# q and k of a forgetting-attention layer projected token-major and turned through DRAM, in a two-layer trunk on one core

## The chip, the cores and the metric

The kernel runs on one core of one Trainium2 chip. The metric is the device time of one execution in microseconds (us), of which three runs are given. A profiled execution is shown besides; its span runs from its first to its last instruction.

## The reference, cut to what matters

Two layers over 256 tokens of width 2048, in float32. Layer 0 mixes tokens with an mLSTM of 4 heads, layer 1 with FoX, a softmax attention of 16 heads of 128 whose logits carry a cumulative log-forget-gate. Each mixer and each SwiGLU feed-forward part (inner width 5632) is preceded by an RMSNorm with a scale and a shift from a conditioning vector, and added to the residual with a gate from the same vector. The part that the change touches:

```python
def fox_mixer(h, w_in, b_f, w_out):
    proj = h @ w_in
    q, k, v, fl = jnp.split(proj, [D_MODEL, 2 * D_MODEL, 3 * D_MODEL], axis=-1)
    heads = lambda a: a.reshape(B, T, Hh, FOX_HEAD_DIM).transpose(0, 2, 1, 3)
    log_f = jax.nn.log_sigmoid(fl + b_f).transpose(0, 2, 1)
    o = forgetting_attention(heads(q), heads(k), heads(v), log_f)
    return o.transpose(0, 2, 1, 3).reshape(B, T, D_MODEL) @ w_out

# forgetting_attention, per head:
#   s = q @ k.T * dh**-0.5 + cum[t] - cum[s], causal;  out = softmax(s) @ v
# swiglu:  (silu(g) * u) @ w_down,  g, u = split(h @ w_gate_up)
```

## The kernel before

All large products run in a split form: a float32 tile is written as hi + lo, both in the fast format of TensorE, and hi·hi, hi·lo and lo·hi are summed in PSUM. Weights come from DRAM in tiles of 4 x 128 rows by 512 columns (1 MB, `fetch`, line 250). For each, `split` (255) lets ScalarE (ACT) cast hi and VectorE (DVE) subtract lo, two 128x1024 pieces each. `raw` tiles have 5 buffers, hi and lo 4 each, so two tiles can be split ahead of TensorE.

Two forms of group multiply the 256 tokens by 512 columns over 16 tiles of the inner dimension:

- `group_a` (316), the plain form. Tokens are stationary, weights move. For each inner tile and each half of the tokens `mm_t` (285) issues three matmuls of 512 columns (lines 288 to 290), 96 a group, into two PSUM banks. The result is token-major: partitions are tokens.
- `group_b` (296), used for q and k of the FoX layer alone. Weights are stationary, activations move. For each inner tile and each of four blocks of 128 output features `mm_b` (269) issues a matmul of 512 columns (line 271; the activation's hi and lo side by side) and one of 256 (line 274), 128 a group, into four banks. The result is feature-major, as attention wants q and k. `total` (366) adds the two halves of each bank: a copy on ACT (368), an add on DVE (370 or 372).

After each weight tile comes a `tick` (245): it runs `adv` waiting steps from the list `steps` and then `bg(n)`, which adds n to a credit. A whole unit of credit fetches a further 1 MB tile of `ada_w` on SP's queue and lets DVE multiply it with the conditioning vector (line 193, the ada products). Weight fetches are on SP's queue too. So one tick is one weight tile: 24 plain matmuls, or 32 of `group_b`. Apart from stretches ordered by hand, the order on each engine is drawn up at compile time from the program order and from what is ready by the compiler's own timing.

The FoX stage (line 1213 on) finishes the v projections begun before, computes the gates, and then runs four iterations (1293): two `group_b` for q and k of four heads, with the v groups of columns 1024 and 1536 ahead of iterations 1 and 2. A head has three steps: *scores* (logit bias, mask and q·k on TensorE, lines 691, 696 and 1229; row maximum on DVE, exponential on ACT, scaling on DVE, line 1251), *flip* (three TensorE transposes of the weights, 958, and their copy on ACT, 959) and *mix* (weights by v, 1261 and 1264, and the split of the result into `y`). The steps of four heads are interleaved and run during the following groups, one a tick, or two a tick in a v group and in the output projection. What is left when the next four heads are added is run at once by `drain`. `project_out` (1093) then runs three plain groups on `y`, running out the steps ahead of the inner tiles from 12 on; the fourth group is in `bridge`.

In the feed-forward parts the products silu(g)·u are token-major and are needed feature-major. One way is by TensorE (`turned`, 342). Where `lag` is set (line 1153: the second chunk of layer 0, both of layer 1) the way is through DRAM: `blocks` (352) has DVE transpose every 32x32 block of a 128x512 tile (353) and POOL write it to `aside` in DRAM (357); `gather` (359) has POOL read it back in four transfers (361) so that each partition holds one feature of each of four blocks; after `lag` ticks, a step `flip` (1165) reads it and casts hi on ACT (1171) and subtracts lo on DVE (1172). In that layout the four feature blocks lie inside, so both read every fourth element.

Tiles of 128x1024 float32 (`slot`) share 16 buffers.

Of the kernel before, what the change touches and what calls it, by code (L numbers as in the profile page):

```python
# [31 lines left out]
def kernel(  # L32
# [26 lines left out]
    def bank():  # L59
        return psum.tile([P, 512], F32, tag="mm", name=nm("mm"))  # L60
# [7 lines left out]
    def t256():  # L68
        return t512()[:, :T]
# [169 lines left out]
    def drain(n=None):  # L239
        if steps:  # L240
            settle()
        for _ in range(len(steps) if n is None else min(n, len(steps))):
            steps.pop(0)()

    def tick(n, adv=1):
        drain(adv)
        grow_all()
        bg(n)
# [17 lines left out]
        raw = fetch(w, k0, nk, c0)  # L266
        return [p for j in range(0, nk, 2) for p in split(raw, j)]

    def mm_b(ps, hi, lo, rhs, first, last):
        def big():  # L270
            nc.tensor.matmul(ps, hi, rhs, start=first, stop=last, skip_group_check=True)  # L271

        def little():
            nc.tensor.matmul(  # L274
                ps[:, T:], lo, rhs[:, :T], start=False, stop=False, skip_group_check=True
            )

        if last:
            little()
            big()  # L280
        else:
            big()
            little()

    def mm_t(ps, hi, lo, act, t, first, last):
        a = act[:, t * P : (t + 1) * P]
        b = act[:, T + t * P : T + (t + 1) * P]
# [4 lines left out]
    def mm_a(ps, hi, lo, act, first, last):  # L292
        for t in range(2):
            mm_t(ps[t], hi, lo, act, t, first, last)

    def group_b(w, nk, c0, act, evac, bgn, adv=1):
        banks = [bank() for _ in range(4)]
        for k in range(0, nk, 4):
            ws = load_w(w, k, 4, c0)
            for m in range(4):  # L300
                cols = slice(m * P, (m + 1) * P)
                for j, (hi, lo) in enumerate(ws):
                    mm_b(
                        banks[m], hi[:, cols], lo[:, cols], act(k + j), k + j == 0, k + j == nk - 1
                    )
                if k + 4 == nk:
                    evac(m, banks[m])
            tick(bgn, adv)

    late = []  # L310

# [39 lines left out]

    def blocks(dst, src, aside):
        nc.vector.transpose(  # L353
            dst.rearrange("p (j b m) -> p j m b", j=4, m=4),
            src.rearrange("p (m j b) -> p j m b", m=4, j=4),
        )
        nc.gpsimd.dma_start(aside, dst)  # L357

    def gather(whole, aside):
        for j in range(4):  # L360
            nc.gpsimd.dma_start(
                whole[32 * j : 32 * j + 32].rearrange("a (g b) m -> a g (b m)", b=32),
                aside.rearrange("t (i a) c -> a (t i) c", a=32)[:, :, j * P : (j + 1) * P],
            )

    def total(ps, out, scale=None):
        b = t256()
        nc.scalar.activation(b, ps[:, T:], AF.Copy, scale=1.0 if scale is None else scale)
        if scale is None:
            nc.vector.tensor_tensor(out, ps[:, :T], b, op=ALU.add)  # L370
        else:
            nc.vector.scalar_tensor_tensor(
                out=out, in0=ps[:, :T], scalar=scale, in1=b, op0=ALU.mult, op1=ALU.add
            )

    def split_act(src, dst):
        nc.scalar.copy(dst[:, :T], src)
# [673 lines left out]
    def interleave(*lists):  # L1051
        return [f for fs in zip(*lists) for f in fs]

    def keep_t(c0, bgn, scale=None, adv=1, layer_w=0):
        if layer_w == 0:
            i = COLS.index(c0)
            unit(i, start[i], KT, bgn)
            sp = SP[i]
            o = slot().rearrange("p (k t) -> p k t", t=T)

            def flip():
                for i in range(2):
                    nc.scalar.copy(o[:, 2 * i : 2 * i + 2, :], turned(sp, i))

            steps.append(flip)
            return o
        o = slot().rearrange("p (k t) -> p k t", t=T)
        group_b(w, KT, c0, h_act, lambda m, ps: total(ps, o[:, m, :], scale), bgn, adv)
        return o

    for i in range(1, 4):
        unit(i, start[i], KT, LR[0])
# [19 lines left out]

    def project_out(wo, res, bgn, adv, upto, norm, w2, heads):
        act = lambda k: act_tile(y, k)
        for i in range(3):
            res.both(i, group_a(
                wo, 512 * i, act, bgn, adv, before=lambda k: drain() if k >= upto else None
            ))
        return bridge(wo, 0, KT, 1536, act, res, 3, norm, w2, heads)

# [10 lines left out]
    def ffn(layer, begun, norm, rates, nsplit=0, srate=0.0, nxt=None):  # L1111
# [36 lines left out]
        def swiglu(gr, lag):  # L1148
            sg = pair(slot())
            banks = column(512 * gr)  # L1150
            for t in range(2):
                nc.scalar.activation(sg[:, t, :], banks[t], AF.Silu)
            banks = column(DFF + 512 * gr)
            for t in range(2):
                nc.vector.tensor_tensor(sg[:, t, :], banks[t], sg[:, t, :], op=ALU.mult)
            first = len(acts)
            acts.extend([None, None])
            if lag:
                whole = slot().rearrange("p (t m) -> p t m", m=4)
                aside = dram.tile([2, P, 512], F32, tag="aside", name=nm("aside"))  # L1160
                for t in range(2):
                    blocks(t512(), sg[:, t, :], aside[t])
                gather(whole, aside)

            def flip(i):
                acts[first + i] = dst = new_act()
                if lag:
                    ps = whole[:, :, 2 * i : 2 * i + 2].rearrange("p t m -> p m t")
                else:
                    ps = turned(sg, i)  # L1170
                nc.scalar.copy(dst[:, :, :T], ps)  # L1171
                nc.vector.tensor_tensor(  # L1172
                    dst[:, :, T:], ps, dst[:, :, :T].bitcast(F32), op=ALU.subtract
                )

            steps.extend([lambda: None] * lag)
            steps.extend([lambda: flip(0), lambda: flip(1)])
# [43 lines left out]
    def fox_head(hd, q, k):  # L1221
        st = {}

        def scores():
            S = abank()
            logits(u3, hd, S, False)
            for t in range(2):
                n = P * (t + 1)
                nc.tensor.matmul(  # L1229
                    S[:, T * t : T * t + n], q[:, t * P : (t + 1) * P], k[:, :n],  # L1230
                    start=False, stop=t == 1, skip_group_check=True,
                )
            mx = small([P, 2], "den", bufs=4)
            buf = slot()
            W = buf[:, : 3 * P]
            st["W"], st["WT"] = W, buf[:, 512 : 512 + 3 * P]
            sm = small([P, 2], "r", bufs=4)
            for t in range(2):
                nc.vector.tensor_reduce(
                    out=mx[:, t : t + 1], in_=S[:, slice(*causal[t])], axis=AX.X, op=ALU.max,  # L1240
                    negate=True,
                )
            for t in range(2):
                nc.scalar.activation(
                    W[:, slice(*packed[t])], S[:, slice(*causal[t])], AF.Exp,
                    bias=mx[:, t : t + 1], accum_out=sm[:, t : t + 1],
                )
            nc.vector.reciprocal(sm, sm)
            for t in range(2):
                wt = W[:, slice(*packed[t])]  # L1250
                nc.vector.tensor_scalar(wt, wt, sm[:, t : t + 1], None, op0=ALU.mult)

        def flip():
            weights_t(st["W"], st["WT"])

        def mix():
            v, WT = vals[hd // 4][:, :, hd % 4 * P : (hd % 4 + 1) * P], st["WT"]
            if hd % 2 == 0:
                y[hd // 2] = new_act()
            O = abank()  # L1260
            nc.tensor.matmul(
                O[:, :T], v[:, 0, :], WT[:, :T], start=True, stop=False, skip_group_check=True
            )
            nc.tensor.matmul(
                O[:, P:T], v[:, 1, :], WT[:, T:], start=False, stop=True, skip_group_check=True
            )
            split_act(O[:, :T], act_tile(y, hd))

        return [scores, flip, mix]
# [22 lines left out]
    u3 = split3(cum, 16, new)  # L1292
    for i in range(4):
        if i == 1:
            vals[2] = keep_v(group_a(w, 2 * D + 1024, h_act, FR, ka=12, banks=begun[2 * D + 1024]))
        if i == 2:
            vals[3] = keep_v(group_a(w, 2 * D + 1536, h_act, FR, 2))
        q = keep_t(512 * i, FR, P ** -0.5, layer_w=1)
        k = keep_t(D + 512 * i, FR, layer_w=1)
        drain()  # L1300
        steps.extend(interleave(*[
            fox_head(4 * i + j, q[:, j, :], k[:, j, :]) for j in range(4)
        ]))
    res = Residual(1, G1, True)
    norm = Norm(res, 1, SC2, SH2)
    begun = project_out(fox_out, res, FR, 2, 12, norm, gate_up[1], [0, DFF, 512])
# [116 lines left out]
```

## Time and profile before

| | |
|---|---|
| runs | 2279.60, 2282.02, 2283.16 us (median 2282.02) |
| profiled execution | 2279.4 us, span 2277.6 us |
| granted TensorE clock, mean | 0.999 |
| TensorE matmul busy | 2255.0 us (99%) |
| TensorE weight load busy | 1848.2 us (81%) |
| VectorE, ScalarE, GpSimd busy | 1653.0, 1139.6, 71.2 us |
| moved by DMA | 640.69 MB, mean 281 GB/s |

The page lists engines as PE (matmul), PEld (weight load, which overlaps PE), DVE, ACT, POOL and SP. A row of a group gives line, engine, operation, what it writes and reads with shapes, the count, busy us, mean ns of one, then the engine's idle time ahead of it and what ended it. Matmul durations overlap; the distance between starts tells the rate. A row of the waits gives who waited for whom, us in total, times and the longest.

### The profile page before, as it was taken

To read this page: it belongs to the slowest core of one execution; us is meant where nothing else is said; L and a number is where in the kernel's file an instruction comes from. 1 tells how busy PE (TensorE), PEld (TensorE's weight loads), DVE (VectorE), ACT (ScalarE), POOL (GpSimd) and SP (SyncE) were. 2 spreads that over 40 slices of the span, in tenths; PEclk is the share of its full clock that TensorE was granted. 3 is DMA by queue.
4 is the path that set the end of the run, shared out by engine and by line. 5 is a ranking of instruction groups with operands and counts; after the bars stand their busy time and mean duration, and the time that the engine had idled before them with its cause. 6 is when DMAs were issued, how large, how long until landed. Compare 5 with 4: busy or idle time off the path is not lost.

```text
span 2277.6 us, 26530 instructions
## 1 busy us (share of the span) xinstructions
PE 2255.0 (99%) x10250; PEld 1848.2 (81%) x10250; DVE 1653.0 (73%) x1865; ACT 1139.6 (50%) x1493; POOL 71.2 (3%) x136
## 2 busy tenths in 40 slices
PE   8999999999999999999999999999999999999998
PEld 5877878888888888888888888887888888888886
DVE  7998789878887878875687777777665555555564
ACT  4778564555543344444555444455444443444443
POOL 1000000000000000100000000000100100010000
PEclk9999999999999999999999999999999999999999
DMA  9998989788888889996667877675777665566662
GB/s 394 371 369 321 353 307 354 283 338 334 325 335 330 326 335 349 360 350 219 217 238 288 299 273 277 250 274 189 271 276 255 221 204 189 201 223 219 206 233 98
DMA packets 93571, 640.69 MB, mean 281 GB/s; under 512 B 11443, under 2 KB 11891, under 8 KB 19077
## 3 DMA queue, kind: packets, MB, share of 16 engines
q1 hardware_dynamic: 86400, 617.79, 73.5%
q0 software_dynamic: 6896, 21.08, 3.1%
q8 instruction: 80, 1.31, 0.2%
q14 instruction: 47, 0.38, 0.0%
q10 hardware_dynamic: 148, 0.14, 0.0%
HBM read 628.44 MB, written 10.52 MB: 281 GB/s over the span
## 4 chain that ended last, share of the span: by engine, by line
PE 87%; DVE 5%; DMA 4%; ACT 2%; issue 1%; POOL 0%; SPq 0%; ACTq 0%; DVEq 0%; POOLq 0%
PE mm L289 25%; PE mm L290 25%; PE mm L288 25%; PE mm L271 5%; PE mm L274 3%; DMA ada<-in_ada_w_dram 3%; DVE lo L262 2%; DVE ada L193 2%; ACT hi L261 1%; DMA slot<-in_w_in_dram 1%; PE aux L1010 0%; PE aux L498 0%; PE aux L1229 0%; PE mm L569 0%; PE mm L565 0%
## 5 line engine op out<-in xcount | busy, mean ns | idle before, releaser
L262 DVE TENSOR_TENSOR lo<-raw,hi 128x1024 fp32r<-128x1024 f32 x764 | 924.2, 1221 | 470.8 <-ACT hi L261 469.5
L261 ACT CAST hi<-raw 128x1024 fp32r<-128x1024 f32 x764 | 796.9, 1054 | 870.7 <-PE mm L290 742.2
L289 PE MATMUL mm<-lo,hT 128*128 128x512 f32 x1846 | 720.3, 390 | 3.3 <-DVE lo L262 3.2
L290 PE MATMUL mm<-hi,hT 128*128 128x512 f32 x1846 | 719.8, 390 | 0.0
L288 PE MATMUL mm<-hi,hT 128*128 128x512 f32 x1846 | 719.1, 392 | 0.0
L193 DVE SCALAR_TENSOR_TENSOR ada<-ada,cs 128x2048 f32<-128x2048 f32 x192 | 438.7, 2285 | 55.7 <-DMA ada<-in_ada_w_dram 55.3
L289 PEld LDWEIGHTS mm<-lo,hT 128*128 128x128 f32 x1846 | 346.7, 188 | 78.5 <-DVE lo L262 7.4
L290 PEld LDWEIGHTS mm<-hi,hT 128*128 128x128 f32 x1846 | 346.5, 188 | 72.4 <-issue 0.5
L288 PEld LDWEIGHTS mm<-hi,hT 128*128 128x128 f32 x1846 | 346.5, 188 | 71.9 <-issue 0.5
L288 PE MATMUL mm<-hi,slot 128*128 128x512 f32 x960 | 375.0, 391 | 0.2 <-ACT slot L1043 0.2
L289 PE MATMUL mm<-lo,slot 128*128 128x512 f32 x960 | 374.2, 390 | 0.2 <-DVE lo L262 0.2
L290 PE MATMUL mm<-hi,slot 128*128 128x512 f32 x960 | 374.1, 390 | 0.0
L288 PEld LDWEIGHTS mm<-hi,slot 128*128 128x128 f32 x960 | 180.3, 188 | 38.0 <-ACT slot L1043 0.8
L290 PEld LDWEIGHTS mm<-hi,slot 128*128 128x128 f32 x960 | 180.2, 188 | 37.7 <-issue 0.7
L289 PEld LDWEIGHTS mm<-lo,slot 128*128 128x128 f32 x960 | 180.2, 188 | 37.5 <-DVE lo L262 0.6
L271 PE MATMUL mm<-hT,hi 128*128 128x512 f32 x512 | 181.5, 401 | 0.0
L274 PE MATMUL mm<-hT,lo 128*128 128x256 f32 x512 | 138.4, 281 | 0.4 <-DVE lo L262 0.4
L271 PEld LDWEIGHTS mm<-hT,hi 128*128 128x128 f32 x512 | 94.4, 188 | 19.6
L274 PEld LDWEIGHTS mm<-hT,lo 128*128 128x128 f32 x512 | 96.6, 189 | 4.1 <-DVE lo L262 1.1
L865 ACT ACTIVATE slot<-mm 128x512 f32<-128x512 f32 x78 | 45.3, 596 | 39.7 <-PE mm L290 37.9
L357 POOL DMA_DIRECT2D aside<-t x32 | 18.0, 562 | 1239.7 <-DVE t L353 1239.7
L1172 DVE TENSOR_TENSOR slot<-slot,slot 128x512 fp32r<-128x512 f32 x32 | 34.8, 1090 | 24.8 <-ACT slot L1171 24.8
(220 smaller groups left out, 1049.6 us busy)
## 6 DMA issues: line engine op xcount, KB each, us to landing
ada<-in_ada_w_dram SPq DMA_DIRECT2D x192, 1024.0 KB, 6.3
raw<-in_gate_up_dram SPq DMA_DIRECT2D x176, 1024.0 KB, 5.2
raw<-in_down_dram SPq DMA_DIRECT2D x88, 1024.0 KB, 4.9
raw<-in_fox_in_dram SPq DMA_DIRECT2D x48, 1024.0 KB, 4.9
raw<-in_w_in_dram SPq DMA_DIRECT2D x44, 1024.0 KB, 7.2
raw<-in_w_out_dram SPq DMA_DIRECT2D x16, 1024.0 KB, 5.8
raw<-in_fox_out_dram SPq DMA_DIRECT2D x16, 1024.0 KB, 4.9
aside<-t POOLq DMA_DIRECT2D x32, 256.0 KB, 2.5
```

Of the source, the lines that this page charges most:

```text
L193: nc.vector.scalar_tensor_tensor(out=raw, in0=raw, scalar=1.0, in1=cs, op0=ALU.mult, op1=ALU.mult, accum_out=acc[layer][:, j : j + 1],)
L261: nc.scalar.copy(hi, raw[:, j : j + 2, :])
L262: nc.vector.tensor_tensor(lo, raw[:, j : j + 2, :], hi.bitcast(F32), op=ALU.subtract)
L271: nc.tensor.matmul(ps, hi, rhs, start=first, stop=last, skip_group_check=True)
L274: nc.tensor.matmul(ps[:, T:], lo, rhs[:, :T], start=False, stop=False, skip_group_check=True)
L288: nc.tensor.matmul(ps, a, hi, start=first, stop=False, skip_group_check=True)
L289: nc.tensor.matmul(ps, a, lo, start=False, stop=False, skip_group_check=True)
L290: nc.tensor.matmul(ps, b, hi, start=False, stop=last, skip_group_check=True)
L357: nc.gpsimd.dma_start(aside, dst)
L865: nc.scalar.activation(SP[i][:, t, :], banks[t], func)
L1172: nc.vector.tensor_tensor(dst[:, :, T:], ps, dst[:, :, :T].bitcast(F32), op=ALU.subtract)
```

## The change

- q and k of the FoX layer are projected by `group_a`. `group_b`, `mm_b` and `total` are gone. ACT copies the two banks out (for q with the factor 1/sqrt(128)), `blocks` and `gather` take them through DRAM into a slot.
- The layout in DRAM and in that slot is now (group of 32 tokens, feature block, token), so that a feature block is read in runs of 32 tokens, 128 elements apart (`tiles`). The feed-forward flips use the same helpers and read such runs too.
- k's slot is read by the score matmul as it lies. q, which is stationary there, is copied on ACT into another slot.
- A list `timed` holds functions with the tick at which they are due. The copy of q is due 6 ticks after the last tick of its k group (4 in the last iteration), which is 10 after its own; the heads' steps are added one tick later, two heads after two heads, and run two a tick. So the heads of iteration i run during the groups of iterations i + 1 and i + 2.
- The v group of columns 1536 comes after the four iterations.
- In the FoX output projection the first two groups run over the inner tiles 0 to 11 first, while the last four heads run, and then over 12 to 15.

```diff
     def blocks(dst, src, aside):
         nc.vector.transpose(
-            dst.rearrange("p (j b m) -> p j m b", j=4, m=4),
+            dst.rearrange("p (j m b) -> p j m b", j=4, m=4),
...
-                whole[32 * j : 32 * j + 32].rearrange("a (g b) m -> a g (b m)", b=32),
+                whole[32 * j : 32 * j + 32].rearrange("a (g c) -> a g c", c=P),
...
+    def tiles(whole):
+        return whole.rearrange("p (g m b) -> p m g b", m=4, b=32)
...
     def tick(n, adv=1):
+        clock[0] += 1
+        while timed and timed[0][0] <= clock[0]:
+            timed.pop(0)[1]()
         drain(adv)
...
     def keep_t(c0, bgn, scale=None, adv=1, layer_w=0):
...
-        o = slot().rearrange("p (k t) -> p k t", t=T)
-        group_b(w, KT, c0, h_act, lambda m, ps: total(ps, o[:, m, :], scale), bgn, adv)
-        return o
+        banks = group_a(w, c0, h_act, bgn, adv)
+        whole = slot()
+        aside = dram.tile([2, P, 512], F32, tag="aside", name=nm("aside"))
+        for t in range(2):
+            own = t512()
+            nc.scalar.activation(own, banks[t], AF.Copy, scale=1.0 if scale is None else scale)
+            blocks(t512(), own, aside[t])
+        gather(whole, aside)
+        return tiles(whole)
...
     def project_out(wo, res, bgn, adv, upto, norm, w2, heads):
+        first = {}
+        if upto == 12:
+            for i in range(2):
+                first[i] = group_a(wo, 512 * i, act, bgn, adv, kb=upto, more=True)
+            assert not timed
+            drain()
         for i in range(3):
             res.both(i, group_a(
-                wo, 512 * i, act, bgn, adv, before=lambda k: drain() if k >= upto else None
+                wo, 512 * i, act, bgn, adv, ka=upto if i in first else 0, banks=first.get(i),
+                before=lambda k: drain() if k >= upto else None,
             ))
...
             def flip(i):
                 acts[first + i] = dst = new_act()
+                hi, lo = dst[:, :, :T], dst[:, :, T:]
                 if lag:
-                    ps = whole[:, :, 2 * i : 2 * i + 2].rearrange("p t m -> p m t")
+                    ps = tiles(whole)[:, 2 * i : 2 * i + 2]
+                    hi, lo = (x.rearrange("p m (g b) -> p m g b", b=32) for x in (hi, lo))
...
                 nc.tensor.matmul(
-                    S[:, T * t : T * t + n], q[:, t * P : (t + 1) * P], k[:, :n],
+                    S[:, T * t : T * t + n].rearrange("p (g b) -> p g b", b=32),
+                    q[:, t * P : (t + 1) * P], k[:, : n // 32],
...
     for i in range(4):
         if i == 1:
-            vals[2] = keep_v(group_a(w, 2 * D + 1024, h_act, FR, ka=12, banks=begun[2 * D + 1024]))
-        if i == 2:
-            vals[3] = keep_v(group_a(w, 2 * D + 1536, h_act, FR, 2))
-        q = keep_t(512 * i, FR, P ** -0.5, layer_w=1)
-        k = keep_t(D + 512 * i, FR, layer_w=1)
-        drain()
-        steps.extend(interleave(*[
-            fox_head(4 * i + j, q[:, j, :], k[:, j, :]) for j in range(4)
-        ]))
+            vals[2] = keep_v(
+                group_a(w, 2 * D + 1024, h_act, FR, 2, ka=12, banks=begun[2 * D + 1024])
+            )
+        far = keep_t(512 * i, FR, P ** -0.5, 2, layer_w=1)
+        k = keep_t(D + 512 * i, FR, None, 2, layer_w=1)
+        q = slot().rearrange("p (m t) -> p m t", t=T)
+        heads = [fox_head(4 * i + j, q[:, j, :], k[:, j]) for j in range(4)]
+
+        def begin(q=q, far=far, heads=heads):
+            nc.scalar.copy(q.rearrange("p m (g b) -> p m g b", b=32), far)
+            timed.append((clock[0] + 1, lambda: steps.extend(
+                interleave(*heads[:2]) + interleave(*heads[2:])
+            )))
+
+        timed.append((clock[0] + (LAND if i < 3 else LAND - 2), begin))
+    vals[3] = keep_v(group_a(w, 2 * D + 1536, h_act, FR, 2))
```

More of the change, by code (lines that the diff above doesn't have):

```diff
@@ L243, in drain @@
             steps.pop(0)()
+    clock = [0]
+    timed = []
     def tick(n, adv=1):
+        clock[0] += 1
+        while timed and timed[0][0] <= clock[0]:
+            timed.pop(0)[1]()
         drain(adv)
@@ L267, in load_w @@
         return [p for j in range(0, nk, 2) for p in split(raw, j)]
[L269 to L283, printed above, removed]
     def mm_t(ps, hi, lo, act, t, first, last):
@@ L294, in mm_a @@
             mm_t(ps[t], hi, lo, act, t, first, last)
[L296 to L308, printed above, removed]
     late = []
@@ L361, in gather @@
             nc.gpsimd.dma_start(
-                whole[32 * j : 32 * j + 32].rearrange("a (g b) m -> a g (b m)", b=32),
+                whole[32 * j : 32 * j + 32].rearrange("a (g c) -> a g c", c=P),
                 aside.rearrange("t (i a) c -> a (t i) c", a=32)[:, :, j * P : (j + 1) * P],
             )
[L366 to L374, printed above, removed]
+    def tiles(whole):
+        return whole.rearrange("p (g m b) -> p m g b", m=4, b=32)
     def split_act(src, dst):
@@ L1052, in interleave @@
         return [f for fs in zip(*lists) for f in fs]
+    LAND = 6
     def keep_t(c0, bgn, scale=None, adv=1, layer_w=0):
@@ L1158, in swiglu @@
             if lag:
-                whole = slot().rearrange("p (t m) -> p t m", m=4)
+                whole = slot()
                 aside = dram.tile([2, P, 512], F32, tag="aside", name=nm("aside"))
@@ L1166, in flip @@
                 acts[first + i] = dst = new_act()
+                hi, lo = dst[:, :, :T], dst[:, :, T:]
                 if lag:
-                    ps = whole[:, :, 2 * i : 2 * i + 2].rearrange("p t m -> p m t")
+                    ps = tiles(whole)[:, 2 * i : 2 * i + 2]
+                    hi, lo = (x.rearrange("p m (g b) -> p m g b", b=32) for x in (hi, lo))
                 else:
                     ps = turned(sg, i)
[L1171 to L1174, printed above, removed]
+                nc.scalar.copy(hi, ps)
+                nc.vector.tensor_tensor(lo, ps, hi.bitcast(F32), op=ALU.subtract)
             steps.extend([lambda: None] * lag)
```

## The prediction

> **What bounds the kernel now.** I read the page first: its busy line, and the line that splits the chain that ended last by engine.
>
> ```profile
> PE 2255.0 (99%) x10250; PEld 1848.2 (81%) x10250; DVE 1653.0 (73%) x1865; ACT 1139.6 (50%) x1493; POOL 71.2 (3%) x136
> ...
> PE 87%; DVE 5%; DMA 4%; ACT 2%; issue 1%; POOL 0%; SPq 0%; ACTq 0%; DVEq 0%; POOLq 0%
> ```
>
> TensorE sets the time, so work taken from the vector engines is worth nothing unless TensorE waits for it. A busy share does not say how densely matmuls follow each other, so I cut stretches: one of plain groups (lines 288 to 290), one in the feed-forward part of each layer, one in the FoX stage. Columns: stretch and length, then busy time and count of PE, PEld, DVE, ACT and POOL, granted clock, DMA share, GB/s.
>
> ```profile
> 1199.97:1211.30 11.33, 11.33 (x51) 9.39 (x50) 8.71 (x9) 5.94 (x9) 0.00 (x0) 1.00 0.82 293
> 850.00:1050.00 200.00, 199.93 (x882) 164.93 (x881) 156.96 (x151) 88.99 (x90) 18.92 (x33) 1.00 0.93 339
> 1600.00:2270.00 670.00, 668.79 (x2950) 553.03 (x2948) 389.72 (x368) 296.44 (x307) 39.27 (x68) 1.00 0.63 216
> 1261.00:1318.00 57.00, 57.00 (x328) 49.07 (x326) 44.63 (x64) 29.77 (x52) 0.00 (x0) 1.00 0.82 305
> ```
>
> A count holds one instruction cut by the edge, so 50 plain matmuls fill 11.33 us: 226.6 ns each, 5.44 us for a step of 24. The form that goes is counted by its line 271 alone (PE and PEld are the two engines shown):
>
> ```profile
> 1215.15:1226.45 11.30, 11.30 (x33) 5.95 (x32) 1.00 0.62 220
> ```
>
> Here 32 whole pairs of lines 271 and 274 fill 11.30 us: 353.1 ns a pair.
>
> **The change, part by part.**
>
> *The q and k projections.* Eight groups in the old form hold 512 pairs, and the page's groups show why a pair is dear:
>
> ```profile
> L271 PE MATMUL mm<-hT,hi 128*128 128x512 f32 x512 | 181.5, 401 | 0.0
> L274 PE MATMUL mm<-hT,lo 128*128 128x256 f32 x512 | 138.4, 281 | 0.4 <-DVE lo L262 0.4
> L271 PEld LDWEIGHTS mm<-hT,hi 128*128 128x128 f32 x512 | 94.4, 188 | 19.6
> L274 PEld LDWEIGHTS mm<-hT,lo 128*128 128x128 f32 x512 | 96.6, 189 | 4.1 <-DVE lo L262 1.1
> ```
>
> A pair streams 768 columns, which at the plain rate is 1.5 x 226.6 = 339.9 ns. Its two weight loads take 188 and 189 ns, and the one beside the 256-column matmul (half of 226.6, 113 ns) does not fit under it. The new groups stream the same columns (96 x 512 = 64 x 768) with 96 loads instead of 128, each under 512 columns. Gain: 512 x (353.1 - 339.9) = 512 x 13.2 ns = **6.8 us**, all of it on TensorE, the path. The low end is no gain, if the new groups run as loosely as the old.
>
> A rule speaks against this. The Trainium skill, "TensorE: Matmul & The Clock Gate", sections "Back-to-back issue gap" and "LDWEIGHTS (loading the stationary operand)", gives N columns N/2.4 + 2.5 ns and a load of 128 columns about 107 ns. An estimate by that page: 215.8 + 109.2 = 325.0 ns for the pair against 323.7 ns for 1.5 plain matmuls, with the loads hidden in both, so 0.7 us over 512 pairs: no change. The trace disagrees: its loads take 188 ns.
>
> *The steps of 16 heads* keep their TensorE instructions. They run two a tick, of two heads in turn, so that a flip comes one tick after its scores; before, it was two or more. The flip needs the head's scaled weights (line 1251), made by VectorE and ScalarE in their order, between splits and ada products. What that adds can be read where heads already ran in pairs. Rows of the timeline: start, length, engine, line.
>
> ```profile
> 1324.84 0.39 PE L691 MATMUL aux<-u,sel 96*128 96x512 bf16 x1
> ...
> 1325.18 0.82 PE L1229 MATMUL aux<-slot,slot 128*128 128x128 f32 x4
> 1325.84 0.38 PE L691 MATMUL aux<-u,sel 96*128 96x512 bf16 x1
> ...
> 1332.19 0.54 DVE L1251 TENSOR_SCALAR slot<-slot,r 128x128 f32<-128x128 f32 x2
> 1332.28 0.39 PE L691 MATMUL aux<-u,sel 96*128 96x512 bf16 x1
> ...
> 1339.72 0.82 PE L958 MATMUL aux<-ident,slot 128*128 128x128 f32 x6
> ...
> 1340.64 0.54 DVE L1251 TENSOR_SCALAR slot<-slot,r 128x128 f32<-128x128 f32 x2
> ...
> 1457.99 0.55 DVE L1251 TENSOR_SCALAR slot<-slot,r 128x128 f32<-128x128 f32 x2
> ...
> 1460.20 0.39 PE L691 MATMUL aux<-u,sel 96*128 96x512 bf16 x1
> ```
>
> After each pair of scores the next step starts just 24 matmuls later. Had it been the flips, the second would be wanted about 0.3 us after that start. First pair: wanted 1332.58, scaled 1332.19 + 0.54 = 1332.73, late 0.15. Second: wanted 1340.02, scaled 1341.18, late 1.16. Third: scaled 1458.54, before 1460.20, in time. The mean, 0.44 us, over eight pairs is 3.5 us; bounds 0 and 8 x 1.16 = 9.3. I take **+1.5 us**, under half the mean, because the compiled order may put ready matmuls of the next tick ahead of a flip that it knows to be late. Behind a late flip on TensorE stand 24 plain matmuls whose splits are done by then. The mix, a tick after the flip, has about 5 us for one copy.
>
> Two heads' scores add 7.44 - 5.44 = 2.00 us to a plain tick (1324.84 to 1332.28). Eight heads ran in such pairs before and sixteen will; for the different breaks between forms I take 0, with a tenth of 2.00 over eight pairs, 1.6 us, either way as an estimate.
>
> *The way of q and k.* Removed per group: four copies (line 368) and four adds. Added: two evacuations of 128x512, two transposes, two writes and four reads issued by POOL; per iteration also the copy of q, 128x1024, on ACT. Nearest groups:
>
> ```profile
> L865 ACT ACTIVATE slot<-mm 128x512 f32<-128x512 f32 x78 | 45.3, 596 | 39.7 <-PE mm L290 37.9
> L361 POOL DMA_DIRECT2D slot<-aside x64 | 37.5, 592 | 64.9 <-DMA aside<-t 43.3 <-ACT hi L261 11.8 <-DMA raw<-in_gate_up_dram 5.8
> L1171 ACT CAST slot<-slot 128x512 fp32r<-128x512 f32 x32 | 35.7, 1118 | 19.9 <-DMA slot<-aside 19.9
> L1172 DVE TENSOR_TENSOR slot<-slot,slot 128x512 fp32r<-128x512 f32 x32 | 34.8, 1090 | 24.8 <-ACT slot L1171 24.8
> ...
> L353 DVE STREAM_TRANSPOSE t<-slot 128x512 f32<-128x512 f32 x32 | 31.8, 1066 | 0.0
> ...
> L368 ACT ACTIVATE t<-mm 128x256 f32<-128x256 f32 x32 | 12.2, 383 | 17.5 <-PE mm L271 17.5
> ```
>
> ACT goes from 4 x 383 to 2 x 596 ns a group, plus a q copy of at most 2 x 1118 every second group. VectorE loses four adds of 256 elements (taken at line 368's 383 ns, the same size) and gains at most 2 x 1066. It was busy 44.63 of 57 us in the FoX stretch, so a fraction of a microsecond per 22 us is hidden: 0. If VectorE's slack were gone, the 16 transposes would cost at most 17 us; the slack excludes that. POOL issues 48 more DMAs at about 0.6 us, with nothing urgent behind them: 0.
>
> *Landing.* The nearest case, in the busiest feed-forward stretch, from the transposes to the read that waited last for the gather:
>
> ```profile
> 863.17 1.98 DVE L353 STREAM_TRANSPOSE t<-slot 128x512 f32<-128x512 f32 x2
> ...
> 884.62 1.14 ACT L1171 CAST slot<-slot 128x512 fp32r<-128x512 f32 x1 [0.47 <-DMA slot<-aside]
> ```
>
> That is 21.5 us. In the new order scores run seven ticks after k's last matmuls (38 us), five for the last four heads (27 us): hidden. The 48 DMAs move 8 x 1.05 MB; over some 180 us that is 47 GB/s on top of 305, about what the stretch at 850 us carried with TensorE idle for 0.07 us. SP's queue fetches as many tiles, in another order in the output projection, and the ada rate a tick stays. I take 0.
>
> *k read in runs of 32 tokens.* No row shows a matmul with such a moving operand. From below 0: the same columns are streamed. From above: if the score matmuls took twice as long, 16 x 0.66 us (line 1229, 1325.18 to 1325.84) = 10.6. I take 0, as a run of 128 bytes is nearer to a whole row than to single elements.
>
> *The squares in the feed-forward parts.* Flips there read runs of 32 instead of every fourth element and should fall below 1118 and 1090 ns, the transposes below 1066. TensorE idled 0.07 and 1.21 us in the two stretches that hold these trips, so the gain is 0, at most 1.2 us. *The output projection* starts two groups up to the last four tiles and ends them after the heads; the same matmuls, 0, bounds ±1 us.
>
> **Sum.** -6.8 + 1.5 = -5.3 us. The profiled execution took 2279.4 us (span 2277.6), so it would take 2274.1. It stands 2.6 below the median of the three runs, 2282.02, at their fast end. Against the median: **2276.7 us**.
>
> **Rivals.**
> - *The late flips eat the gain.* From 6.8/8 = 0.85 us a pair the change is worth nothing; at 1.16 in every pair the time is 2282 - 6.8 + 9.3 = 2284.5. For it: the second pair. Against: the third, and the freedom to reorder.
> - *Slower: an ada wait lands in front of the second head's scaling in every pair.* VectorE works in order, and in the stage it stood at ada transfers this often (total, times, longest):
>
> ```profile
> DVE ada L193 <- DMA ada<-in_ada_w_dram: 23.1, 18, 3.6
> ```
>
>   The new transfers make ada land later. With the mean wait, 23.1/18 = 1.28 us, on top of 1.16, a pair costs 2.44: 2282 - 6.8 + 19.5 = 2294.7. It decides from (6.8 + 4.6)/8 = 1.42 us a pair. Against it: 18 waits fall over some 49 ticks, not at eight chosen ones.
> - *k's runs at half rate*: 2282 - 6.8 + 1.5 + 10.6 = 2287.3. Nothing in the trace speaks for it.
> - *The change doesn't do what it says, as the pair is no dearer:* about 2281.3 if loads hide as the cited page has it; the pair's 353.1 ns speaks against it.
> - *More:* no late flip, the breaks 1.6 less and 1.2 in the feed-forward parts: 2282 - 9.6 = 2272.4.
>
> **How the numbers follow.** About 0.2%, 4.6 us, is what a measurement of this kernel can tell from no change; the bounds are 2277.4 and 2286.6. The sum as forecast (2274 to 2279.5) has 0.58, of which 0.50 is below 2277.4; more gain 0.07; late flips 0.19, all within; no dearer pair 0.03; k at half rate 0.04 and the ada waits 0.09, both slower. So faster 0.57, within 0.30 (0.08 + 0.19 + 0.03), slower 0.13. The range is 2271 to 2285.5: from the case of more gain, less 1.4 for the spread of the runs, to past the late flips; it leaves out the slower cases. The likeliest alone: 2274 to 2279.5.
>
> **What would show it.** Right: plain matmuls about 227 ns apart in the q and k groups; steps of two heads 2.0 us above a plain tick; ScalarE and VectorE never waiting for a gather in the stage; feed-forward flips shorter with the same TensorE time. Wrong: TensorE idle ahead of line 958's or 1229's successors, matmuls of the scores over 0.66 us, or idle at splits because evacuations and the q copy stand before them.

## The result, and the profile after

| | before | changed |
|---|---|---|
| median, same chip | 2279.84 us (6 runs) | 2297.20 us (6 runs, 2292.29 to 2308.47) |
| ratio, 95% interval | | 1.0081 [1.0057, 1.0105] |
| profiled execution | 2279.4 us, span 2277.6 us | 2300.37 us, span 2298.6 us |
| granted clock, mean | 0.999 | 0.996 |

The change makes the kernel 0.8% slower, against a forecast of 2276.7 us. Line numbers have moved: the plain matmuls are lines 278 to 280 (were 288 to 290), the hi and lo splits 267 and 268, the scores' q·k 1213, row maximum 1224, exponential 1229, reciprocal 1233, scaling 1236, the flips' transposes 927 and their copy 928, the reads of the gather 337. The ada product is still line 193, its fetch line 192.

The page of the changed kernel: the busy line, the chain that ended last, the group of ada products, and one DMA row (the last number is the median from issue to landing; it was 4.9 before).

```profile
PE 2257.5 (98%) x9994; PEld 1840.0 (80%) x9994; DVE 1629.1 (71%) x1849; ACT 1127.7 (49%) x1481; POOL 98.9 (4%) x184
...
PE 82%; DMA 8%; DVE 6%; ACT 2%; issue 2%; SPq 0%; ACTq 0%; DVEq 0%
...
L193 DVE SCALAR_TENSOR_TENSOR ada<-ada,cs 128x2048 f32<-128x2048 f32 x192 | 438.9, 2286 | 86.2 <-DMA ada<-in_ada_w_dram 86.0
...
raw<-in_fox_in_dram SPq DMA_DIRECT2D x48, 1024.0 KB, 6.7
```

VectorE has less to do (1629.1 against 1653.0 us) and the chain goes less through TensorE, twice as much through DMA (8% against 4%). To place it I cut the FoX stage in both kernels, from the gates' product to the first transposes of `bridge`. The columns are those of the prediction's stretches: before, then changed, then a stretch of a changed q group with nothing late in it.

```profile
1211.53:1543.99 332.46, 330.45 (x1750) 279.25 (x1749) 247.37 (x341) 161.87 (x272) 0.00 (x0) 1.00 0.75 274
```

```profile
1212.52:1565.08 352.56, 331.85 (x1495) 269.95 (x1493) 244.89 (x325) 164.55 (x260) 27.76 (x48) 0.98 0.81 282
1216.15:1238.80 22.65, 22.65 (x101) 18.77 (x100) 17.19 (x23) 14.24 (x19) 0.00 (x0) 1.00 0.76 273
```

The stage takes 352.56 instead of 332.46 us, +20.1; what follows it takes 733.5 and 733.6 us and what precedes it 1.0 more, so nearly all of the loss is here. The third row is the part that went as planned: 100 plain matmuls in 22.65 us, 226.5 ns each, in a q group. TensorE stood still for 20.7 us of the stage (352.56 - 331.85; before 2.0), and some of its busy time was slow: the clock of 0.98 is an average over three short windows at half.

Who waited in the stage (waiting engine and line, what for, then us in total, times, longest): before, then changed.

```profile
DVE ada L193 <- DMA ada<-in_ada_w_dram: 26.9, 19, 3.9
```

```profile
DVE ada L193 <- DMA ada<-in_ada_w_dram: 56.3, 23, 6.9
...
PE aux L927 <- DVE slot L1236: 16.2, 6, 5.6
...
PE mm L279 <- DVE lo L268: 4.2, 3, 1.6
```

TensorE waits six times for the scaling of a head and three times for a lo split, 20.4 us in all. Both are VectorE's, and VectorE waits twice as long as before for ada tiles. The weight tiles of the stage land later too (6.4 us on average against 5.1 before), but no row has an engine waiting for a weight tile of the FoX projections. The largest of the six, in the timeline (start, length, engine, line; idle time ahead and what ended it in brackets):

```profile
1327.47 0.33 SPq L192 DMA_DIRECT2D ada<-in_ada_w_dram  x1
...
1327.87 0.82 PE L1213 MATMUL aux<-slot,slot 128*128 128x128 f32 x4
...
1328.67 2.34 POOL L337 DMA_DIRECT2D slot<-aside  x4 [5.96 <-DMA aside<-t]
...
1333.98 0.49 PE L927 MATMUL aux<-ident,slot 128*128 128x128 f32 x3
...
1337.15 2.29 DVE L193 SCALAR_TENSOR_TENSOR ada<-ada,cs 128x2048 f32<-128x2048 f32 x1 [5.63 <-DMA ada<-in_ada_w_dram]
...
1339.45 1.20 DVE L268 TENSOR_TENSOR lo<-raw,hi 128x1024 fp32r<-128x1024 f32 x1
...
1340.57 0.54 DVE L1236 TENSOR_SCALAR slot<-slot,r 128x128 f32<-128x128 f32 x2
...
1340.99 0.45 PE L927 MATMUL aux<-ident,slot 128*128 128x128 f32 x1 [5.59 <-DVE slot L1236]
...
1342.95 0.63 PE L279 MATMUL mm<-lo,hT 128*128 128x512 f32 x1
...
1343.37 0.63 PE L280 MATMUL mm<-hi,hT 128*128 128x512 f32 x1
1343.80 0.63 PE L278 MATMUL mm<-hi,hT 128*128 128x512 f32 x1
```

Read it downwards. An ada tile is fetched at 1327.47. At 1328.67 POOL issues the four reads of a gather, and the tile lands only ahead of 1337.15, some 9.7 us after its fetch. VectorE, which takes its work in order, stands for 5.63 us at the product, then does it (2.29), a lo split (1.20) and only then the second head's scaling. TensorE has flipped the first head at 1333.98 and idles for 5.59 us in front of the second head's flips. After that it is slow: matmuls start 425 ns apart instead of 227. The window of half clock:

```profile
1339.60:1346.40 6.80, 5.41 (x15) 4.29 (x16) 2.65 (x4) 1.52 (x2) 0.00 (x0) 0.50 0.87 316
```

There are three of these in the stage (6.8, 3.4 and 3.4 us), with TensorE busy for 11.63 us of them. At 425 ns for 227, some 47% of that is lost, 5.4 us. TensorE's busy time in the stage grew by only 1.4 us (331.85 - 330.45), so without the half clock it would be 4.0 less than before: that is what the plain form brought here of its 6.8. With 18.7 us more of standing still (20.7 - 2.0), the sum is 18.7 + 5.4 - 4.0 = 20.1 us.

### The profile page after: what moved, and what is told of

The parts are those of the page before. It is cut to its first block, busy times and chain, and to the rows that moved or that the text cites. A ratio compares the mean times of both kernels' runs of the same rounds, so it can differ in the third digit from the quotient of the medians.

```text
span 2298.6 us, 26114 instructions
## 1 busy us (share of the span) xinstructions
PE 2257.5 (98%) x9994; PEld 1840.0 (80%) x9994; DVE 1629.1 (71%) x1849; ACT 1127.7 (49%) x1481; POOL 98.9 (4%) x184
## 4 chain that ended last, share of the span: by engine, by line
PE 82%; DMA 8%; DVE 6%; ACT 2%; issue 2%; SPq 0%; ACTq 0%; DVEq 0%
PE mm L280 26%; PE mm L279 26%; PE mm L278 26%; DMA ada<-in_ada_w_dram 7%; DVE ada L193 2%; DVE lo L268 2%; ACT hi L267 1%; DMA slot<-in_w_in_dram 1%; PE aux L979 0%; PE aux L467 0%; PE mm L538 0%; PE aux L322 0%; PE mm L534 0%; PE mm L535 0%; PE aux L927 0%
## 5 line engine op out<-in xcount | busy, mean ns | idle before, releaser
L279 PE MATMUL mm<-lo,hT 128*128 128x512 f32 x2102 | 822.6, 391 | 7.7 <-DVE lo L268 7.5
L278 PE MATMUL mm<-hi,hT 128*128 128x512 f32 x2102 | 822.5, 393 | 0.0
L280 PE MATMUL mm<-hi,hT 128*128 128x512 f32 x2102 | 822.3, 391 | 0.0
L279 PEld LDWEIGHTS mm<-lo,hT 128*128 128x128 f32 x2102 | 396.2, 189 | 94.0 <-DVE lo L268 12.8
L280 PEld LDWEIGHTS mm<-hi,hT 128*128 128x128 f32 x2102 | 396.0, 188 | 82.6 <-issue 0.5
L278 PEld LDWEIGHTS mm<-hi,hT 128*128 128x128 f32 x2102 | 395.9, 188 | 81.7 <-issue 0.5
L333 POOL DMA_DIRECT2D aside<-t x48 | 27.0, 563 | 1165.2 <-DVE t L329 1164.6
L834 ACT ACTIVATE slot<-mm 128x512 f32<-128x512 f32 x78 | 45.2, 595 | 39.7 <-PE mm L280 37.9
L337 POOL DMA_DIRECT2D slot<-aside x96 | 56.2, 592 | 133.8 <-DMA aside<-t 52.1
L417 ACT ACTIVATE t<-X 128x512 f32<-128x512 f32 x32 | 20.2, 631 | 41.0 <-DVE X L412 41.0
L1158 DVE TENSOR_TENSOR slot<-slot,slot 128x512 fp32r<-128x512 f32 x32 | 21.9, 688 | 20.7 <-ACT slot L1157 20.7
L1136 ACT ACTIVATE slot<-mm 128x512 f32<-128x512 f32 x44 | 25.5, 598 | 14.9 <-PE mm L280 14.5
L412 DVE TENSOR_TENSOR X<-X,t 128x512 f32<-128x512 f32 x48 | 32.3, 687 | 0.5
```

Of the source, the lines that this page charges most:

```text
L278: nc.tensor.matmul(ps, a, hi, start=first, stop=False, skip_group_check=True)
L279: nc.tensor.matmul(ps, a, lo, start=False, stop=False, skip_group_check=True)
L280: nc.tensor.matmul(ps, b, hi, start=False, stop=last, skip_group_check=True)
L337: nc.gpsimd.dma_start(whole[32 * j : 32 * j + 32].rearrange("a (g c) -> a g c", c=P), aside.rearrange("t (i a) c -> a (t i) c", a=32)[:, : ...
L412: nc.vector.tensor_tensor(cols, cols, m, op=ALU.add)
L834: nc.scalar.activation(SP[i][:, t, :], banks[t], func)
```

## The experiments

My theory after this look: the transfers of q and k (4.2 MB written, 4.2 MB read back in pieces of 512 bytes) make the 1 MB loads land later, VectorE stands at the ada product, and what queues behind it (scalings, lo splits) is late for TensorE. The rivals: *spacing*, that heads two a tick bring the flip too close behind the scores whatever the transfers do; *plain groups*, that the shorter steps leave VectorE no slack; and *the reads in a burst*, four at a time. Each ratio below is to the kernel before, run on the same chip; the medians come from several chips, so ratios are the better comparison between runs.

**The changed kernel without its transfers.** q and k are constants then; the matmuls, evacuations, transposes (`turn` is the transpose of `blocks` alone) and steps remain.

```diff
-            blocks(t512(), own, aside[t])
-        gather(whole, aside)
+            turn(t512(), own)
+        nc.gpsimd.memset(whole, 0.25)
```

> The changed kernel without the 48 DMAs of q and k through DRAM: evacuations and transposes stay, and GpSimd fills the slot with a constant, so the attention of the FoX layer works on constant q and k. The order of the heads stays as changed. Theory T: ada tiles land in 5 us again (median 5.95, largest 11.3 in the changed kernel), VectorE's waits for ada fall from 54 to about 23 us, flips wait under 4 us in all, no half clock: 2297 - 25 = 2272 us. Rival S: the flips are still late, over 10 us in all, and the time stays at 2288 or above.

Measured: 2276.76 us (11 runs, 2274.2 to 2281.55), ratio 0.9991 [0.9982, 1.0000]. The stage and its waits:

```profile
1212.40:1539.00 326.60, 324.38 (x1494) 266.28 (x1493) 246.69 (x325) 165.14 (x260) 4.77 (x5) 1.00 0.76 278
```

```profile
DVE ada L193 <- DMA ada<-in_ada_w_dram: 19.1, 17, 3.4
...
PE aux L930 <- DVE slot L1238: 1.1, 2, 0.7
```

With VectorE's work and the spacing of the heads unchanged, the stage falls by 26.0 us to 5.9 below before, flips wait 1.1 us and the clock stays full. The transfers are the cause: without them neither the spacing nor the plain groups make the kernel slower. The 26.0 us are of two single executions, the fastest of these 11 (2274.2 us) and one of the changed kernel above its median; by the medians the transfers cost 20.4 us (2297.20 - 2276.76), and by the ratios 0.9%.

**The kernel before with the 48 transfers added**, unused: the old groups, layout and one head a tick.

```diff
         group_b(w, KT, c0, h_act, lambda m, ps: total(ps, o[:, m, :], scale), bgn, adv)
+        whole = slot().rearrange("p (t m) -> p t m", m=4)
+        aside = dram.tile([2, P, 512], F32, tag="aside", name=nm("aside"))
+        for t in range(2):
+            nc.gpsimd.dma_start(aside[t], o[:, 2 * t : 2 * t + 2, :].rearrange("p m t -> p (m t)"))
+        gather(whole, aside)
```

> The kernel before with the 48 transfers added and unused: after each q or k group its tile is written to DRAM and read back by the same helper into a slot that nothing reads. Old groups, old order of the heads. Theory T: ada landing goes up to 9 to 11 us where it overlaps, VectorE's waits for ada go from 27 to about 55 us, but as flips come two or more ticks after their scores TensorE stands under 6 us more, mostly at splits: 2280 to 2287 us. If the transfers alone make the time, it reaches 2295.

Measured: 2301.74 us (2301.26 to 2306.41), ratio 1.0095 [1.0081, 1.0109].

```profile
DVE ada L193 <- DMA ada<-in_ada_w_dram: 65.3, 26, 6.7
...
PE aux L1266 <- DVE slot L378: 7.7, 2, 5.6
PE mm L274 <- DVE lo L262: 4.2, 9, 1.3
```

This is above the 2280 to 2287 us that I expected: the transfers alone make the kernel before as slow as the change did, its stage 352.1 us. There are no close flips there, so other work is late: the mixes' splits (one waits 5.6 us, with 6.8 us of half clock around it) and nine lo splits. The victim depends on the order of steps; the wait at ada is no shorter (65.3 us against 56.3). So the loss does not need the new *spacing*.

**Writes without reads.** The changed kernel with the gather's reads replaced by a constant.

```diff
-        gather(whole, aside)
+        nc.gpsimd.memset(whole, 0.25)
```

> The changed kernel with the writes of q and k to DRAM, but without the reads back (GpSimd fills the slot with a constant, so the FoX attention works on constant q and k). It tells which half of the transfers is felt. If the reads, in pieces of 512 bytes, are what makes the big loads late: like e2_no_transfers, 2274 to 2279 us, ada waits under 30 us. If the writes count as much: halfway, 2284 to 2290 us.

Measured: 2280.19 us (11 runs, 2275.39 to 2283.16), ratio 0.9990 [0.9979, 1.0002]; the profiled stage 335.3 us. From issue to landing for ada tiles in the stage (smallest, median, largest, us): before, changed, writes only, no transfers.

```profile
DMA to landing us min/median/max: 4.7/4.9/6.6
```

```profile
DMA to landing us min/median/max: 4.7/5.9/11.3
```

```profile
DMA to landing us min/median/max: 4.6/5.7/8.2
```

```profile
DMA to landing us min/median/max: 4.7/5.8/7.1
```

The median does not tell the last three apart; the largest does. A product that comes just in time is held up by the latest of them. The loads of the stage (ada and weights) whose landing is on record can be sorted by whether they were in flight together with a transfer of POOL's: in the changed kernel the 35 that were took 7.55 us on average and the 24 that weren't 5.32 (before: 5.07 for all 62); with writes only, 6.73 for 17 and 5.64 for 44. A long load is likelier to meet a transfer, so this overstates what the transfers do; over all these loads the mean is 6.64 us in the changed kernel and 5.64 without the transfers. In the profiled stages the writes alone cost 8.7 of the 26.0 us (335.3 - 326.6), but over all executions this run is not told from the one without transfers (0.9990 against 0.9991), and its median lies between the two ranges that I expected. So the reads bring most of the loss; that the writes alone cost anything is not shown.

**The reads one a tick** instead of four at once. `piece` is one of the four reads of `gather`, and `due` runs it j ticks later.

```diff
-        gather(whole, aside)
+        for j in range(4):
+            if j == 0:
+                piece(whole, aside, j)
+            else:
+                due(j, lambda j=j: piece(whole, aside, j))
```

> The changed kernel with the four reads of each gather issued one a tick instead of all at once. Same bytes, same order of the heads. Theory T with the burst as its cause: big loads that overlap a gather land in about 6 us instead of 7.6 on average and none in 11, VectorE waits for ada 30 to 40 us instead of 56, 2280 to 2286 us. If what counts is the sum of the traffic, landing times and waits stay and the time stays at 2292 to 2300.

Measured: 2294.39 us (2293.58 to 2299.54), ratio 1.0063 [1.0051, 1.0076]; stage 343.9, TensorE held at flips for 11.7 us, three windows of half clock. Spreading takes little of the loss away (the two intervals overlap), so the burst is not the heart of it.

**The ada product a tick after its fetch** in the stage, so that it would find its tile landed. `take(n)` runs the products of all fetched tiles but the last n; in the stage `ahead[0]` is 1.

```diff
+            coming.append((layer, v, k, ada_tile(layer, v, k)))
+            take(ahead[0])
```

> The changed kernel, but in the FoX stage up to the output projection each ada product runs one tick after its fetch instead of right behind it; transfers and the order of the heads stay as changed. Theory T (the path from the transfers to the flips leads through VectorE's place in front of an ada tile): landing times stay long, VectorE's waits for ada fall below 20 us, flips wait under 5 us: 2275 us. Rival S: flips still late by over 10 us, 2288 or above. A third: the five weight buffers are held a tick longer, SP fetches weights later, and splits become late instead: 2285 to 2300 with the idle at splits.

Measured: 2295.60 us (2285.35 to 2301.61), ratio 1.0070 [1.0052, 1.0088]. A miss. In the profiled execution, its fastest, VectorE waited 44.1 us at ada and TensorE 9.3 us at five flips:

```profile
DVE ada L197 <- DMA ada<-in_ada_w_dram: 44.1, 24, 5.4
...
PE aux L941 <- DVE slot L1251: 9.3, 5, 3.5
```

A later product didn't give a longer lead: from the issue of a fetch to its product 6.6 us passed on average, against 7.0 in the changed kernel. The likely reason is that a fetch on SP's queue waits for a buffer and the buffers are freed by the same late VectorE. In the changed kernel SP's queue waited for VectorE ahead of ada fetches most of all at the ada products themselves:

```profile
SPq L192 <- DVE ada L193: 68.3, 14, 10.8
```

**Four heads interleaved** as before, two steps a tick.

```diff
-                interleave(*heads[:2]) + interleave(*heads[2:])
+                interleave(*heads)
```

> The changed kernel with the steps of four heads in turn again (a flip two ticks after its scores, as mostly before), all else as changed. In the changed kernel TensorE stood about 17.5 us at flips, 5 us at late splits, and about 5 us went to half clock after the long idles. Theory T (the new transfers double the landing of ada tiles, VectorE stands in front of them in its order, and the flips that come one tick after their scores pay): the ada waits stay (about 50 us of VectorE idle in the stage), the flips no longer meet them, the half clock goes; 2297 - 17.5 - 5 = 2275 us, late splits stay. Rival S (the spacing of one tick is late by itself, with or without the transfers): 2275 too. If TensorE still stands over 8 us at flips, more than the spacing is wrong, and the time stays above 2285.

Measured: 2291.08 us (2286.60 to 2292.46), ratio 1.0049 [1.0036, 1.0062].

```profile
DVE ada L193 <- DMA ada<-in_ada_w_dram: 78.0, 29, 6.1
...
PE aux L660 <- ACT slot L1229: 5.7, 4, 3.0
PE aux L927 <- ACT slot L1229: 3.5, 5, 1.5
```

The flips no longer wait for the scaling, but the loss moves: scores and flips now wait for a PSUM bank that the exponentials (line 1229) have not yet emptied, behind row maxima that VectorE makes late. VectorE's own wait has grown (78.0 us against 56.3). The time stays far above the 2275 us of both theories: this order takes the loss from 0.8% to 0.5%, and the two intervals overlap.

**Fewer ada products in the iterations.** The rate is 0.95 a tick ahead of the four iterations and after them, and 0.38 within, instead of 0.66 throughout. In the traces 25 products start in the stage instead of 31: of the other six, one comes ahead of it and five behind.

```diff
-    FR = CFG["fr"]
+    FR = 0.95
...
+    FR = 0.38
     for i in range(4):
...
+    FR = 0.95
     res = Residual(1, G1, True)
```

> The changed kernel with the ada work of the FoX stage moved off the ticks that carry the transfers: 0.95 tiles a tick before and behind the four iterations and 0.38 during them, against 0.66 throughout; about the same sum. Transfers and order of the heads as changed. Theory T: fewer ada tiles for VectorE to stand at, and less traffic beside the gathers: ada waits under 25 us, flips wait under 5 us, 2273 to 2278 us, faster than the kernel before. Rival: any transfer beside the weights makes the splits late, and the ada tiles are not the cause: 2288 or above, with the idle at splits.

Measured: **2274.35 us** (2272.07 to 2275.25), ratio 0.9968 [0.9956, 0.9979]: faster than both kernels.

```profile
1211.90:1539.30 327.40, 324.83 (x1495) 266.44 (x1495) 231.50 (x308) 164.90 (x260) 27.77 (x48) 1.00 0.81 282
```

```profile
DVE ada L193 <- DMA ada<-in_ada_w_dram: 26.7, 13, 6.0
...
PE aux L927 <- DVE slot L1236: 1.8, 3, 1.2
...
PE mm L279 <- DVE lo L268: 0.7, 1, 0.7
```

All 48 transfers are there (POOL 27.77 us), yet the stage is 25.2 us shorter than the changed kernel's, within 0.8 of that without transfers. Slow loads are there too: an ada tile still takes up to 10.6 us to land (11.3 in the changed kernel). What has gone is most of the meeting of heads, transfers and ada products on VectorE's queue: VectorE starts 308 instructions in the stage instead of 325, and its wait at ada is that of before. The run does not tell apart the fewer products from the fewer loads.

**Both, rate and spread reads.** The two edits above together.

> Both of the former together: reads of a gather one a tick, ada work 0.95, 0.38 and 0.95 a tick. Theory T: at least as good as each alone, about 2273 us (the kernel before less the 6.8 us of the plain groups). Rival: no better than the better one of the two.

Measured: 2274.48 us (2271.30 to 2276.24), ratio 0.9970 [0.9958, 0.9982]: nothing on top of the rate alone.

**The control: the kernel before at the same rates.** The three lines of the rate in the kernel before.

> The kernel before with the ada work moved as in e6_rate (0.95, 0.38, 0.95 tiles a tick) and nothing else: the control for e6_rate, which took 2274.4 us. If e6_rate's gain is the plain groups' (theory T: 6.8 us less, once nothing waits), this stays at 2278 to 2281 us. Rival: the ada rate alone was the gain, then 2274 us.

Measured: 2277.42 us (11 runs, 2275.99 to 2278.26), ratio 0.9984 [0.9975, 0.9993]; stage 330.0 us. So about half of what the fast version has comes from the rate, which helps either kernel. The rest, 0.9968 against 0.9984, would be the change itself: 0.16%, 3.6 us; but the two intervals overlap slightly, so it is not clear of noise. The profiled stages differ by 2.6 us (330.0 - 327.4). TensorE's busy time in them differs by 5.1 us (329.96 - 324.83), near the 6.8 of the plain form; the fast version gives half of that back by standing still for 2.6 us, where this control never does.

**Plain groups alone.** The kernel before with `group_a` for q and k, the result laid into the slot as it comes, so that attention works on a wrong layout.

```diff
-        group_b(w, KT, c0, h_act, lambda m, ps: total(ps, o[:, m, :], scale), bgn, adv)
+        banks = group_a(w, c0, h_act, bgn, adv)
+        for t in range(2):
+            nc.scalar.activation(
+                o[:, 512 * t : 512 * t + 512], banks[t], AF.Copy, scale=1.0 if scale is None else scale
+            )
...
```

> The kernel before with plain groups for q and k and nothing else of the change: ACT copies both banks, still token-major, into the slot that attention reads, so the attention works on tiles of the wrong layout (no transposes, no transfers, old order of the steps). It measures the disputed gain alone. The prediction's term: 512 x 13.2 ns = 6.8 us, 2280 - 6.8 = 2273 us. Rival G (the new groups run as loosely as the old, splits or evacuations come late): 2280 us.

Measured: 2277.44 us (11 runs, 2275.17 to 2283.89), ratio 1.0000 [0.9991, 1.0008]. No gain can be read from this one. Its profiled execution (2283.55 us, near the top of its range) shows a stage of 331.9 us, in which a mix waited 3.1 us for VectorE, with 3.4 us of half clock:

```profile
1317.76 2.29 DVE L193 SCALAR_TENSOR_TENSOR ada<-ada,cs 128x2048 f32<-128x2048 f32 x1 [1.54 <-DMA ada<-in_ada_w_dram]
...
1320.45 1.22 PE L1265 MATMUL aux<-slot,slot 128*128 128x256 f32 x2 [3.12 <-DVE slot L378]
```

In this execution TensorE's busy time in the stage is 3.8 us less than before (330.45 - 326.67), and 5.2 us of standing still eat it up. Here a drained head met VectorE late even without transfers; whether that is what takes the gain from the other executions is not shown.

**The squares' layout alone**, in the kernel before: `tiles(whole)` and the regrouped hi and lo of `flip`.

> The kernel before with the new layout of the squares in the feed-forward parts alone; q and k as before. The prediction: flips on ACT and VectorE fall below 1118 and 1090 ns, transposes below 1066 ns, the time stays (at most 1.2 us less, 2279 to 2281 us). Rival: the shorter reads free raw buffers earlier and move the order of the loads, over 4 us either way.

Measured: 2278.68 us (11 runs, 2277.44 to 2282.07), ratio 0.9992 [0.9983, 1.0001]. Its groups with the new layout:

```profile
L1177 DVE TENSOR_TENSOR slot<-slot,slot 128x512 fp32r<-128x512 f32 x22 | 15.1, 688 | 11.4 <-ACT slot L1176 11.4
L353 DVE STREAM_TRANSPOSE t<-slot 128x512 f32<-128x512 f32 x22 | 14.2, 684 | 0.0
...
L1176 ACT CAST slot<-slot 128x512 fp32r<-128x512 f32 x22 | 13.6, 620 | 12.3 <-DMA slot<-aside 12.3
```

All three are 36 to 45% shorter than the prediction's rows (1118, 1090 and 1066 ns), and it moves nothing that can be told from no change, as TensorE waits for none of it.

## Why the prediction was wrong

- **The plain form's gain: right where nothing waits.** The q groups run at 226.5 ns a matmul. In the stage TensorE's busy time is 6.1 us less than before without the transfers (330.45 - 324.38), and 5.1 less between the two kernels at the moved rates. The stage without transfers came out 5.9 us below before, against a sum of 5.3 (6.8 less 1.5), though that execution is the shortest of its 11. The rule of the Trainium skill that I weighed ("TensorE: Matmul & The Clock Gate", "Back-to-back issue gap" and "LDWEIGHTS (loading the stationary operand)"), by which the two forms cost the same, is not what this stretch shows. Over all executions the gain is smaller and less sure: 0.09% without the transfers, 0.16% beside the control, none in the run of plain groups alone.
- **"Landing ... I take 0": this step failed.** I priced 48 transfers by mean bandwidth, 47 GB/s on top of 305, and compared it with a stretch of the feed-forward part that carried as much while TensorE idled for 0.07 us. The total was no worse, but the comparison left out who is waiting: that stretch has no heads, so no short chain through VectorE that TensorE needs within a tick. What counts is the latency of the single loads that such a chain stands behind: up to 11.3 us for an ada tile beside the transfers, 7.1 without them. I asked only whether q and k land in time for the heads, which they did. What I left out of the sum is what they delay on the way: 20.4 us between the medians with and without the transfers, 26.0 between the profiled stages. The prediction did say in a rival that the new transfers make ada land later, but the sum has no term for it.
- **The late flips: 1.5 us taken, bounds 0 to 9.3; measured 16.2**, with 4.2 us of lo splits that had no term. The reason for taking under half the mean, that the compiled order may put ready matmuls ahead of a late flip, gave nothing: VectorE's wait for a DMA is not in the compiled order, and TensorE stood at the flips. Without the transfers the term is 1.1 us, close to the forecast; so the step's own price was fair and its neighbour's was missing.
- **The half clock had no term**: 5.4 us. The prediction's trace granted 1.00 in each stretch that it showed, as TensorE never stood long there.
- **The rival with the ada wait in front of the second head's scaling** (0.09; 2294.7) is the mechanism that came. Its place and direction were right; it struck six flips rather than every pair, at 2.7 us each (16.2/6) and not 2.44. It had neither the half clock nor the late splits, so that its 2294.7 comes near the measured 2297.20 is partly luck. Its 18 waits of before were held against it as they fall over 49 ticks; but the transfers run during the very ticks in which the heads do.
- **k in runs of 32 tokens: right at 0.** Score matmuls of before (line 1229) and changed (1213):

```profile
L1229 PE MATMUL aux<-slot,slot 128*128 128x128 f32 (+1 forms) x64 | 13.1, 327 | 0.0
```

```profile
L1213 PE MATMUL aux<-slot,slot 128*128 128x128 f32 (+1 forms) x64 | 13.1, 327 | 0.0
```

- **The way of q and k on ACT and VectorE, the squares, POOL's issues: right at 0.** No row of the changed kernel has ACT or TensorE waiting for a gather of q or k; the squares are hidden, as their run alone shows.

## What to carry to other kernels

Price an added transfer by what it does to the landing of loads that others need just in time, not by its share of the bandwidth; then ask which in-order engine stands at such a load and what short chain queues behind it. A stretch that carries the same bytes is a comparison only if it has the same chain. If the loads can be moved out of the ticks with the chain, as the rate of ada products could, the loss goes; what is left of the gain is then small (0.16% beside the control) and not clear of noise.

## What the runs showed of the hardware

- TensorE's granted clock halves around short idles. The windows in the changed kernel, from 1339.56, 1383.93 and 1441.96 us, lasted 6.8, 3.4 and 3.4 us and came with idles of 5.59, 3.81 and 2.29 us; one of 1.81 us brought none. The last three of these idles (the first is shown above):

```profile
1384.48 0.88 PE L927 MATMUL aux<-ident,slot 128*128 128x128 f32 x3 [3.81 <-DVE slot L1236]
```

```profile
1407.08 0.30 PE L927 MATMUL aux<-ident,slot 128*128 128x128 f32 x1 [1.81 <-DVE slot L1236]
```

```profile
1440.49 1.07 PE L927 MATMUL aux<-ident,slot 128*128 128x128 f32 x6 [2.29 <-DVE slot L1236]
```

  The Trainium skill ("TensorE: Matmul & The Clock Gate", "HAM oscillation — how this bites in real kernels") sets the limit at gaps of about 3.4 us; here 2.29 us was enough. The length alone does not decide: with the reads one a tick an idle of 1.51 us was followed by half clock (from 1310.40 us), and with the product a tick later one of 3.50 us (1330.56 to 1334.06) was not. The windows keep a beat of 3.413 us: the three starts are 13 and 17 beats apart, each lasts one or two, and in the other runs with several windows in the stage the starts are whole beats apart too. What within a beat brings the half clock was not settled.
- Transfers that raise the DMA share of the stage from 0.76 to 0.81 lengthen the mean of its loads from 5.64 to 6.64 us, and the largest for an ada tile from 7.1 to 11.3. How much of it is the reads' small pieces and how much their bytes stays open.
- Runs of 32 elements instead of every fourth: 1118 to 620 ns on ScalarE and 1090 to 688 on VectorE, for 128x512. The transpose of 32x32 blocks, which wrote with that stride before, went from 1066 to 684.
